# What a product costs on the clock that orders a chain of transformer layers

## The chip, the cores and the metric

The kernel runs on one core of a Trainium2 chip. The metric is the device time of one execution in microseconds (us); the figure given is the median of three executions. TensorE (PE) does the matrix products, VectorE (DVE), ScalarE (ACT) and GpSimd (POOL) the elementwise work, SyncE (SP) issues most of the transfers. Each engine runs its own instructions strictly in the order in which the program was written for it, and waits for other engines by semaphores.

## The reference, cut to what matters

512 tokens of 1024 features pass through two blocks; all of it is in float32.

```
f = swiglu(rms_norm(h)) ;  h += 0.5 * rms_norm(f)            # feed-forward, width 2816
u = rms_norm(h) @ w_in                                        # mixing
h += rms_norm(concat(norm(stick_breaking(u)), norm(chunk_band(u))) @ w_out)
f = swiglu(rms_norm(h)) ;  h += 0.5 * rms_norm(f)
h += rms_norm((p @ w_ple_proj) * sigmoid(h @ w_ple_gate))     # gated embedding (PLE)
x = h
x += conv_mixer(rms_norm(x)) ; x += fox_attention(rms_norm(x))
x += gated_delta_rule(rms_norm(x)) ; x += windowed_attention(rms_norm(x))
return rms_norm(x)
```

The gated delta rule works in chunks of 64 tokens and inverts a triangular 64x64 matrix for each head and chunk. What follows a norm can't start before the sum over all features of the layer before is there; these are the places where the program has a chain of small steps between two large products.

## The kernel before, in words

Activations lie feature-major, 128 features on the partitions and 512 tokens along the columns. Each large product (GEMM) multiplies a 128x128 weight block with up to 512 columns. Weights and activations are split into a high and a low part, so that a float32 product is three products of a faster type; one such triple is the unit in which the GEMM loops (`gemm`, L689; `vproj`, L745) work. A weight block is loaded by SP, its high part is copied out by ACT, its low part subtracted by DVE (`load_to`, L637).

The rest of the network is written as generators. A norm has the steps `stats` (L820: products of one column that sum over partitions, then a square root on ACT and a few small operations on DVE), `rows` (L842: a transpose that spreads the factor over the partitions) and, after a block whose output is normed, `post_norm`: for each of 8 feature tiles a scaling on DVE, a residual addition to `h` on DVE or POOL, a copy on ACT, a split on DVE and a square whose sum POOL or DVE takes. It ends with the next norm's `stats` and `rows`. In what follows, g is the step that scales and adds, g2 the norm behind it; both are done for two halves of 256 tokens. Attention heads and the heads of the delta rule (`head`, L1683) are longer generators of the same kind; the latter's triangular inverse uses products of 32x32 (`mm32`, L1772).

What interleaves all this is a rough clock, kept while the program is written. `free["PE"]` is its time on PE; each product adds its assumed cost there (`product`, L658, called by `mm`, L669, and `transpose`, L684). Operations of the other engines wait in a list and are written when their turn comes by the clock (`next_op`, L336; `Eng.call`, L366 on, holds their assumed costs: a line in the number of columns for each engine). After each triple of GEMM products `poll` (L566) looks at the generators: a generator's next step is written as soon as what it needs has been ready by the clock for 150 ns:

```
if t.ready + MARGIN <= free["PE"]:
    t.step()
```

So the costs decide nothing but order: how many GEMM products stand ahead of a step on PE, and what stands ahead of an operation on DVE, ACT and POOL. Work in products narrower than the array is also counted up (`thin`), and past a limit of 900 ns GEMM products that could run go first.

In the profile nearly all operations of DVE, ACT and POOL have line L391 (the helper that issues them), products L682 and transposes L687.

Of the kernel before, what the change touches and what calls it, by code (L numbers as in the profile page):

```python
# [13 lines left out]
PSUM = bass.MemoryType.PSUM  # L14

# functions of the activation tables, in the order in which they are looked for
TABLES = {0: (AF.Exp, AF.Tanh), 3: (AF.Sqrt,), 5: (AF.Ln,), 6: (AF.Ln, AF.Exp), 9: (AF.Sin,), 18: (AF.Silu, AF.Tanh, AF.Sin)}
P = 128
S = 512
# [3 lines left out]
# tiles whose sums after a norm are taken off the vector engine  # L23
# [7 lines left out]
# column tiles of the delta rule's projections for each head, and the gates projected after them  # L31
GDN_QKV = {j: [m + j for m in (0, 8, 16) if m + j != 1 and j < 8] for j in range(1, 9)}
GDN_Z = {j: [24 + i for i in z] for j, z in zip(range(1, 9), ((), (), (), (0,), (1,), (2,), (3,), (4, 5, 6, 7)))}
# column tiles of the windowed attention: keys, queries and gates
# [4 lines left out]
def _weights_plan():  # L39
    """Order in which the 128x128 weight blocks are used: (weight, k tile, column tile); or a block of the last  # L40
    columns, 32 of each of 4 k tiles: (weight, NARROW, number)."""
# [95 lines left out]
def _constants():  # L137
    """Constants of the shapes: matrices of 128 rows, side by side."""
# [4 lines left out]
    # sums over the later keys, and over the earlier tokens  # L143
# [4 lines left out]
    # joins of blocks of b rows within 32: the odd row blocks at the even column block before  # L148
# [14 lines left out]
class Loan:  # L163
    """Gives a place back when the last view of it is gone."""
# [37 lines left out]
def chain_kernel(ctx, tc, xT, pT, wall, params, consts, chbias, pos, out):  # L202
# [8 lines left out]
    # Each engine runs its instructions in the order of tracing, so that order decides how well they overlap.  # L211
    # A rough clock is kept while tracing. The products are traced as they come and advance it. What the other
    # engines are given waits in `pending` and is traced when its turn comes by that clock: inputs there, engine
    # free. free[e]: when engine e has done what was traced; at[tile][part]: when a part of a tile is there;
    # used[tile][part]: when its last use ends.
# [5 lines left out]
    # what a task's inputs should be there before its products  # L221
    MARGIN = 150.0
    # time of products in parts of the array since others; too many in a row let its clock drop
# [8 lines left out]
    def name(x):  # L232
        """Of the place that a tile is in."""
        return place_of.get(x.name, x.name)

    def parts(ap):
        """The 128-column parts of a tile that are touched, and the elements per partition."""
        w = ap.ap[0][0]
        lo = hi = ap.offset % w if w > 1 else 0
        n = 1  # L240
        for st, c in list(ap.ap)[1:]:
            hi += abs(st) * (c - 1)
            n *= c
        return range(lo // P, hi // P + 1), n

    # from the end of an instruction to the start of one that waits for it
# [8 lines left out]
    def there(ap, key):  # L255
        """When a tile's part can be read by an engine."""
# [5 lines left out]
    def unused(ap, key):  # L262
        """When it can be written."""
# [23 lines left out]
    class Op:  # L287
        """An instruction of an engine other than the tensor engine."""
# [14 lines left out]
        def load(self):  # L303
            """The table to load first."""
# [31 lines left out]
    def next_op():  # L336
        """The pending instruction that can start first, and when."""
# [20 lines left out]
    class Eng:  # L358
# [6 lines left out]
        def __getattr__(self, op):  # L365
            f = getattr(self.eng, op)  # L366

            def call(*a, **kw):
# [19 lines left out]
                else:  # L388
                    a0, a1 = (258, 3.34) if ptr else self.POOL.get(op, (147, 2.1))
                    cost = a0 + a1 * n  # L390
                Op(self.key, lambda: f(*a, **kw), outs, ins, cost, self.prio, func, more)  # L391
# [3 lines left out]
    def both():  # L395
        """Has the table of exp and ln loaded, in its turn."""
# [8 lines left out]
    # for what has time, and for what others wait for  # L405
# [4 lines left out]
    class Places:  # L410
        """Tiles of a size, lent for as long as a view of them is kept."""
# [4 lines left out]
        def close(self):  # L416
            """Gives the free ones back, and each of the others when its loan ends."""
            self.of.free.extend(self.free)
            self.free = self.of.free
# [5 lines left out]
        def take(self, n):  # L425
            """Some of the places, for a task alone."""
# [14 lines left out]
    class Slot:  # L441
        """A place whose tiles differ in type."""
# [22 lines left out]
    def room(n):  # L465
        """Whether a task can take places, with some left for others."""
# [5 lines left out]
    class Row(dict):  # L472
        """Tiles by number, there from their first use on."""
# [20 lines left out]
    # Generators hold chains of products. They yield what their next products wait for: tiles, a number of  # L494
    # banks, another task, a condition. Products of the running GEMM fill that time.
# [5 lines left out]
    def ready_at(y):  # L501
        if y is None:
            return 0.0
        if isinstance(y, int):  # one bank more stays for the GEMM, if it is not the one that waits
# [39 lines left out]
    def go_on(until=NEVER):  # L544
        """The next event: an instruction of another engine or a task's step, if before a time."""
# [20 lines left out]
    def poll(on=None):  # L566
        """Run what is ready; what gets ready until the tiles `on` are there."""
# [38 lines left out]
    def roots():  # L606
        """Has the table of roots loaded before it is needed."""
        A.activation(dull, eps, AF.Sqrt)

# [1 line left out]
    # chunks loaded ahead: more before the engines are busy with norms, and then fewer  # L611
# [7 lines left out]
    def load(i):  # L619
# [3 lines left out]
        if PLAN[i][0][1] == NARROW:  # L623
            # both parts of each k tile's columns side by side
# [6 lines left out]
        # soon needed, or not  # L631
# [36 lines left out]

# [1463 lines left out]
```

## Time and profile before

| | |
|---|---|
| time, median of 3 | 2178.8 us (2176.52 to 2179.45) |
| span of the profiled execution | 2180.4 us (no other time is given for that execution) |
| PE busy | 2125.1 us (97%), 13647 records |
| DVE, ACT, POOL busy | 1310.0 (60%), 991.7 (45%), 291.0 us (13%) |
| mean granted TensorE clock | 0.993 |

The profile shows one execution. "Busy" is the time in which an engine had an instruction under way. In a timeline, neighbouring instructions of one form are joined in a row (x12 is 12 of them); in square brackets stands how long the engine idled before the row and which engine let it go on. The granted clock (PEclk) is 1.00 where TensorE runs at 2.4 GHz and 0.50 where it runs at 1.2 GHz.

### The profile page before, as it was taken

What the parts mean: (1) busy time and instruction counts of PE and PEld (TensorE: products, weight loads), DVE (VectorE), ACT (ScalarE), POOL (GpSimd) and SP (SyncE); (2) the same over time, 40 slices, a digit from 0 to 9 for tenths busy, and PEclk for the clock granted to TensorE, in tenths of its full rate; (3) what the DMA queues carried; (4) which work ended last, traced back from release to release, by engine and by line L of the source; (5) the groups of instructions that cost most, each with busy time, mean ns of one, the idle gap of its engine ahead of it and who ended that gap; (6) DMA issues with size and microseconds to landing.
All of it is one profiled execution on the core that took longest, in us unless ns stands there. A gap on an engine that the chain in (4) does not pass through costs nothing.

```text
span 2180.4 us, 35912 instructions
## 1 busy us (share of the span) xinstructions
PE 2125.1 (97%) x13647; PEld 1783.3 (82%) x13647; DVE 1310.0 (60%) x2755; ACT 991.7 (45%) x2167; POOL 291.0 (13%) x596
## 2 busy tenths in 40 slices
PE   8999999999999999999989999999998999999998
PEld 6888889878889888889988887888877777778777
DVE  5433455757767442455775554256568677665896
ACT  5332343566766332333643234344446554533764
POOL 0000001210103000000120012000015242222320
PEclk9999999999999999999999999999999999999999
DMA  5332241211231332332323223322222212223221
GB/s 168 97 97 94 96 138 58 64 61 55 87 102 45 108 115 74 100 111 79 93 73 97 97 89 112 122 64 67 70 85 69 60 55 55 64 83 89 81 83 59
DMA packets 105405, 186.13 MB, mean 85 GB/s; under 512 B 12392, under 2 KB 18952, under 8 KB 105232
## 3 DMA queue, kind: packets, MB, share of 16 engines
q1 hardware_dynamic: 103920, 179.62, 26.7%
q0 software_dynamic: 1312, 4.21, 0.6%
q8 instruction: 107, 1.75, 0.3%
q14 instruction: 66, 0.54, 0.1%
HBM read 179.03 MB, written 2.13 MB: 83 GB/s over the span
## 4 chain that ended last, share of the span: by engine, by line
PE 83%; DVE 10%; POOL 3%; issue 2%; ACT 2%; DMA 1%; SPq 0%; DVEq 0%; POOLq 0%; ACTq 0%
PE ps L682 81%; DVE t L391 8%; PE ps L687 2%; POOL b L391 2%; ACT t L391 1%; DVE h L391 1%; POOL t L391 1%; DVE b L391 1%; DMA wst<-in_wall_dram 0%; DMA h<-in_xT_dram 0%; ACT L391 0%; DVE pad L391 0%; SPq L391 0%; POOL h L391 0%; DVE a L391 0%
## 5 line engine op out<-in xcount | busy, mean ns | idle before, releaser
L682 PE MATMUL ps<-t,t 128*128 128x512 f32 (+6 forms) x10712 | 2046.1, 353 | 18.3 <-DVE t L391 9.9
L682 PEld LDWEIGHTS ps<-t,t 128*128 128x128 f32 (+2 forms) x10712 | 1684.2, 186 | 320.4 <-issue 28.0
L391 DVE TENSOR_TENSOR t<-wst,t 128x512 fp32r<-128x512 f32 (+1 forms) x646 | 446.7, 717 | 255.9 <-ACT t L391 254.5
L391 ACT ACTIVATE t<-t 128x512 f32<-128x512 f32 (+4 forms) x450 | 248.7, 566 | 614.6 <-DVE t L391 604.2
L391 ACT ACTIVATE t<-wst 128x512 fp32r<-128x512 f32 (+1 forms) x646 | 381.0, 622 | 95.6 <-DMA wst<-in_wall_dram 93.7
L391 DVE TENSOR_TENSOR t<-ps,t 128x512 f32<-128x512 f32 (+2 forms) x247 | 155.4, 639 | 299.9 <-PE ps L682 297.9
L391 DVE TENSOR_TENSOR t<-t,t 128x512 fp32r<-128x512 f32 (+4 forms) x367 | 225.3, 625 | 68.2 <-ACT t L391 62.3
L391 ACT ACTIVATE t<-ps 128x512 f32<-128x512 f32 (+5 forms) x357 | 143.4, 418 | 255.6 <-PE ps L682 171.9
L391 POOL TENSOR_TENSOR t<-t,t 128x512 f32<-128x512 f32 (+1 forms) x99 | 119.9, 1212 | 543.0 <-ACT t L391 464.5
L391 POOL TENSOR_TENSOR h<-h,t 128x256 f32<-128x256 f32 x40 | 34.1, 860 | 798.3 <-DVE t L391 796.7
L391 ACT ACTIVATE t<-t,a 128x257 f32<-128x257 f32 (+5 forms) x128 | 66.2, 519 | 45.2 <-DVE a L391 42.7
L391 ACT ACTIVATE t<-h,prm 128x256 fp32r<-128x256 f32 (+1 forms) x80 | 46.3, 588 | 81.2 <-DVE h L391 70.2
L391 DVE SCALAR_TENSOR_TENSOR t<-h,prm,t 128x256 fp32r<-128x256 f32 (+1 forms) x80 | 65.0, 826 | 8.8 <-ACT t L391 8.8
L391 DVE SCALAR_TENSOR_TENSOR t<-pad,prm,t 128x512 f32<-128x512 f32 (+1 forms) x92 | 68.6, 753 | 0.8
L687 PE MATMUL ps<-cst,t 128*128 128x128 f32 x400 | 63.1, 279 | 2.8 <-DVE t L391 2.0
L391 ACT ACT_TABLE_LOAD x48 | 61.6, 1283 | 6.1 <-DVE a L391 4.5
L687 PEld LDWEIGHTS ps<-cst,t 128*128 128x128 f32 x400 | 48.7, 143 | 15.2 <-DVE t L391 3.3
L391 ACT ACTIVATE t<-h 128x256 f32<-128x256 f32 (+2 forms) x112 | 49.5, 466 | 22.6 <-DVE h L391 20.3
L391 POOL TENSOR_SCALAR b<-b 128x4 f32<-128x4 f32 (+3 forms) x84 | 23.2, 276 | 231.1 <-DVE b L391 226.0
L682 PEld LDWEIGHTS ps<-t 32*32 32x32 f32 (+1 forms) x2304 | 33.1, 109 | 24.4 <-DVE t L391 10.3
L391 DVE TENSOR_SCALAR t<-t,a 128x256 f32<-128x256 f32 (+3 forms) x128 | 49.2, 394 | 2.1
L682 PE MATMUL ps<-t 32*32 32x32 f32 (+1 forms) x2304 | 41.0, 197 | 7.1 <-DVE t L391 6.8
(93 smaller groups left out, 670.6 us busy)
## 6 DMA issues: line engine op xcount, KB each, us to landing
wst<-in_wall_dram SPq DMA_DIRECT2D x644, 256.0 KB, 2.7
t<-t SPq DMA_DIRECT2D x40, 64.0 KB, 2.0
h<-in_xT_dram SPq DMA_DIRECT2D x8, 256.0 KB, 5.3
t<-in_chbias_dram POOLq DMA_DIRECT2D x8, 256.0 KB, 3.1
t<-cdr POOLq DMA_DIRECT2D x8, 256.0 KB, 5.7
t<-gdr SPq DMA_DIRECT2D x32, 64.0 KB, 3.8
out_dram<-t SPq DMA_DIRECT2D x16, 128.0 KB, 1.8
cst<-in_consts_dram SPq DMA_DIRECT2D x1, 626.0 KB, 6.3
```

What stands on the lines that cost most here:

```text
L391: Op(self.key, lambda: f(*a, **kw), outs, ins, cost, self.prio, func, more)
L682: PE.matmul(ps, lhsT, rhs, start=start, stop=stop, **kw)
L687: PE.transpose(ps, src, idn)
```

## The change

No instruction is added or taken out: both programs have the same 11800 products and the same operations on the other engines. What changes is the table of costs by which the clock runs. A product's cost without the new term for array parts:

| product | columns | cost before, ns | cost after, ns |
|---|---|---|---|
| split float32 (GEMM) | 512 | 215.8 | 226.7 |
| split float32 (GEMM) | 256 | 109.2 | 120.0 |
| split float32 | 128 | 215.8 | 226.7 |
| float32 | 128 | 215.8 | 220.0 |
| float32 | 32 | 109.2 | 220.0 |
| transpose | 128 | 107.0 | 110.0 |
| 32x32 of the inverse | 32 | 34 | 25 |

New is `changed`: 95 ns more for a product that uses another part of the array (32, 64 or 128 rows by 32, 64 or 128 columns) than the product before it. On the other engines, an instruction on 32 to 127 partitions costs 115 ns more. Explicit costs (`tile=`) change for the sums of norms, gates, the weighing in attention, the stick-breaking values and the products of the inverse. Comments were taken out as well, and line numbers shift (L391 to L393, L682 to L697, L687 to L702).

```
+                if op != "dma_start" and any(32 <= x.ap[0][1] < P for x in outs + ins):
+                    cost += 115
                 Op(self.key, lambda: f(*a, **kw), outs, ins, cost, self.prio, func, more)
...
+    mode = [(P, P)]
+    CHANGE = 95.0
+
+    def changed(rows, cols):
+        new = tuple(next(x for x in (32, 64, P) if n <= x) for n in (rows, cols))
+        if new == mode[0]:
+            return 0.0
+        mode[0] = new
+        return CHANGE
+
     def mm(ps, lhsT, rhs, start=True, stop=True, tile=None, **kw):
         ps, lhsT, rhs = raw(ps), raw(lhsT), raw(rhs)
-        n = max(parts(rhs)[1], 64)
+        n = parts(rhs)[1]
         if tile is not None:
             ns = tile
         elif rhs.dtype == F32:
-            ns = 4 * n / 2.4 + 2.5
+            ns = 2 * max(110.0, (2 * n + 8) / 2.4)
         elif rhs.dtype == F32R:
-            ns = (n if n >= 256 else 4 * n) / 2.4 + 2.5
+            ns = ((n if n >= 256 else 4 * n) + 32) / 2.4
         else:
-            ns = n / 2.4
+            ns = max(n, P) / 2.4 + 2.5
+        ns += changed(rhs.ap[0][1], parts(lhsT)[1])
         thin[0] = max(0.0, thin[0] + (ns if tile is not None else -0.5 * ns))
...
-        product(ps, (src, idn), 107.0)
+        product(ps, (src, idn), 110.0 + changed(P, P))
...
-                   skip_group_check=True, tile=187)
+                   skip_group_check=True, tile=220)
...
-                       start=j == 0, stop=j == n // P - 1, skip_group_check=True, tile=134 if len(heads) > 1 else None)
+                       start=j == 0, stop=j == n // P - 1, skip_group_check=True, tile=110 if len(heads) > 1 else None)
...
-                       tile=0.95 * (S - kt * P))
+                       tile=0.84 * (S - kt * P))
...
-                        mm(ps[gs, cs], lhsT[gs, cs], rhs[gs, cs], tile=34)
+                        mm(ps[gs, cs], lhsT[gs, cs], rhs[gs, cs], tile=25)
...
-                    mm(p5[b, cs], nL[a, c * P + b.start : c * P + b.stop], Tm[a, cs], tile=34)
+                    mm(p5[b, cs], nL[a, c * P + b.start : c * P + b.stop], Tm[a, cs], tile=40)
...
-                mm(p8[64:P, cs], nL[0:64, c * P + 64 : c * P + P], T64[0:64, cs], tile=50)
+                mm(p8[64:P, cs], nL[0:64, c * P + 64 : c * P + P], T64[0:64, cs], tile=124)
```

How the order moves is counted on PE by the GEMM products that stand ahead of a step, and three places show it. In the names, ps is a PSUM bank, cst the table of constants, b a small tile, h the residual stream, prm the gains and t any other tile; the last number only counts tiles, and differs between the two programs for one and the same tile.

The first place is PE at the end of the first feed-forward layer, first half of the tokens: the `stats` of g2 are the products of one column (128x1).

```order
L682 MATMUL ps_236<-t_7_2929,t_5_2698 128x256
L682 MATMUL ps_237<-t_6_2924,t_5_2698 128x256
L682 MATMUL ps_237<-t_6_2924,t_6_2699 128x256
L682 MATMUL ps_237<-t_7_2929,t_5_2698 128x256
L682 MATMUL ps_241<-t_6_2924,t_5_2698 128x256
L682 MATMUL ps_241<-t_6_2924,t_6_2699 128x256
L682 MATMUL ps_241<-t_7_2929,t_5_2698 128x256
L682 MATMUL ps_239<-cst,t_8_2925 128x1 x2
L682 MATMUL ps_240<-t_6_2924,t_5_2698 128x256
```

```order
L697 MATMUL ps_235<-t_6_2305,t_2_2674 128x256
L697 MATMUL ps_235<-t_6_2305,t_2_2675 128x256
L697 MATMUL ps_235<-t_6_2306,t_2_2674 128x256
L697 MATMUL ps_235<-t_7_2383,t_2_2674 128x256
L697 MATMUL ps_235<-t_7_2383,t_2_2675 128x256
L697 MATMUL ps_235<-t_7_2384,t_2_2674 128x256
L697 MATMUL ps_236<-cst,t_8_2922 128x1 x2
L697 MATMUL ps_235<-t_4_2461,t_2_2674 128x256
L697 MATMUL ps_235<-t_4_2461,t_2_2675 128x256
```

Before, the products of the next layer's first column tiles (t_6_2924, the operand just made) already stand ahead of the sums; after, the last products of the feed-forward layer's second half still follow them. Between the `rows` of g and these `stats` stand 108 products of 256 columns before and 99 after.

The second place is DVE in the second half of the same stretch, just ahead of that half's `stats` of g2: operations out of `wst` are the low parts of weight blocks, those on h and prm the splits of the next operand, and those out of ps with one other tile evacuate products.

```order
L391 TENSOR_TENSOR t_3_3308<-wst_248,t_4_3307 128x512
L391 SCALAR_TENSOR_TENSOR t_7_2952<-h_255,prm,t_9_2943 128x256
L391 SCALAR_TENSOR_TENSOR t_5_3219<-t_4_1608,b_166,ps_235 128x256
L391 SCALAR_TENSOR_TENSOR t_9_2969<-h_256,prm,t_8_2947 128x256
L391 TENSOR_TENSOR t_6_3334<-wst_249,t_6_3333 128x512
L391 SCALAR_TENSOR_TENSOR t_7_3329<-ps_236,t_4_3194 128x256
L391 TENSOR_TENSOR t_8_3330<-ps_237,t_4_3194 128x256
L391 SCALAR_TENSOR_TENSOR t_3_3331<-ps_241,t_4_3194 128x256
L391 TENSOR_TENSOR t_7_3357<-wst_246,t_7_3356 128x512
L391 SCALAR_TENSOR_TENSOR t_4_2975<-h_257,prm,t_9_2960 128x256
```

```order
L393 SCALAR_TENSOR_TENSOR t_7_2949<-h_255,prm,t_9_2940 128x256
L393 TENSOR_TENSOR t_9_3292<-wst_247,t_6_3291 128x512
L393 SCALAR_TENSOR_TENSOR t_4_3213<-t_4_1608,b_166,ps_236 128x256
L393 SCALAR_TENSOR_TENSOR t_9_2966<-h_256,prm,t_8_2944 128x256
L393 TENSOR_TENSOR t_4_3316<-wst_248,t_6_3315 128x512
L393 SCALAR_TENSOR_TENSOR t_4_3337<-ps_237,t_4_3168 128x256
L393 TENSOR_TENSOR t_3_3338<-ps_241,t_4_3168 128x256
L393 SCALAR_TENSOR_TENSOR t_4_2972<-h_257,prm,t_9_2957 128x256
```

One weight subtraction that stood ahead of the last scaling (the operation with b_166) stands behind it now, and one that stood ahead of the last split (h_257) stands behind that.

The third place is PE in the delta rule, where the first 32x32 products of head 0 stand among the GEMM products of the projections.

```order
L682 MATMUL ps_240<-t_33_13897,t_32_14425 128x512
L682 MATMUL ps_240<-t_23_13916,t_36_14526 128x512
L682 MATMUL ps_240<-t_23_13916,t_36_14527 128x512
L682 MATMUL ps_240<-t_22_13917,t_36_14526 128x512
L682 MATMUL ps_235<-t_28_14465 32x32 x16
L682 MATMUL ps_240<-t_21_13919,t_36_14526 128x512
```

```order
L697 MATMUL ps_238<-t_25_13897,t_22_14375 128x512
L697 MATMUL ps_238<-t_23_13916,t_27_14406 128x512
L697 MATMUL ps_238<-t_23_13916,t_30_14407 128x512
L697 MATMUL ps_238<-t_20_13917,t_27_14406 128x512
L697 MATMUL ps_240<-t_36_14451 32x32 x16
L697 MATMUL ps_238<-t_23_13919,t_27_14406 128x512
```

The neighbours look alike, but what stands ahead differs: between the score products of head 1 and these 32x32 products lie 45 GEMM products before and 33 after.

The same count at the other places of which the prediction speaks, as GEMM products by which a step stands earlier than before: in the exit of the first feed-forward layer 3 at its first `rows`, 12 at the first `stats` of g2, 6 at the second `rows` of g, 30 at the second `stats` of g2 and 24 at the last `rows`; in that of the second feed-forward layer 6 at its first step, 6 to 9 at the second half's `stats` and `rows` of g, and 24 at its last `rows`; in that of the gated embedding 3 at its first `rows`, 12 at the `stats` of the second half, and 27 at its last `rows` (all of 256 columns). At the end of the delta rule's output product 3 at the `stats` and 6 at the `rows` (of 512 columns). In the attention stages a step stands earlier by 1.1 us of PE work on average in the mixing layer and by 2 us in the windowed attention, counted with the durations of the trace before.

## Rows read from the trace of the kernel before

**Rows 1.** The page: busy time and share of the span, and the chain that ended last.
```profile
PE 2125.1 (97%) x13647; PEld 1783.3 (82%) x13647; DVE 1310.0 (60%) x2755; ACT 991.7 (45%) x2167; POOL 291.0 (13%) x596
...
PE 83%; DVE 10%; POOL 3%; issue 2%; ACT 2%; DMA 1%; SPq 0%; DVEq 0%; POOLq 0%; ACTq 0%
```

**Rows 2.** Busy time by stretch: PE, PEld, DVE, ACT, POOL, granted clock, DMA.
```profile
200.00:300.00 100.00, 100.00 (x443) 82.81 (x442) 47.43 (x73) 30.16 (x54) 0.00 (x0) 1.00 0.31 100
358.00:405.00 47.00, 43.01 (x351) 41.82 (x350) 37.85 (x87) 24.14 (x57) 22.63 (x28) 1.00 0.25 74
657.00:700.00 43.00, 39.23 (x320) 38.08 (x319) 36.59 (x84) 25.29 (x62) 21.03 (x24) 1.00 0.18 57
1085.00:1126.00 41.00, 34.90 (x275) 34.09 (x274) 35.45 (x81) 23.93 (x52) 19.21 (x24) 0.96 0.18 52
1640.00:1930.00 290.00, 279.09 (x3709) 222.50 (x3709) 201.34 (x509) 148.26 (x475) 99.58 (x271) 0.99 0.23 63
1660.00:1690.00 30.00, 24.52 (x439) 18.31 (x439) 28.25 (x66) 11.10 (x40) 15.94 (x32) 0.93 0.22 63
2050.00:2140.00 90.00, 88.41 (x569) 68.08 (x569) 79.31 (x257) 63.04 (x168) 23.14 (x53) 1.00 0.24 71
```

**Rows 3.** PE's timeline at the exit of the first feed-forward layer.
```profile
361.10 13.19 PE L682 MATMUL ps<-t,t 128*128 128x256 f32 x108
375.36 0.61 PE L682 MATMUL ps<-cst,t 128*128 128x1 f32 x4 [1.07 <-POOL t L391]
...
381.20 0.38 PE L687 MATMUL ps<-cst,b 128*128 128x128 f32 x2
381.33 9.10 PE L682 MATMUL ps<-t,t 128*128 128x256 f32 x73
...
395.59 2.30 PE L682 MATMUL ps<-t,t 128*128 128x256 f32 x17 [1.11 <-DVE t L391]
397.73 0.50 PE L682 MATMUL ps<-cst,t 128*128 128x1 f32 x4
```

**Rows 4.** POOL's timeline in the same stretch.
```profile
395.98 0.73 POOL L391 TENSOR_TENSOR t<-t,t 128x256 f32<-128x256 f32 x1 [0.99 <-ACT t L391]
```

**Rows 5.** DVE's timeline there: a weight subtraction, and a split beside POOL and alone.
```profile
391.51 1.23 DVE L391 TENSOR_TENSOR t<-wst,t 128x512 fp32r<-128x512 f32 x1
392.66 0.95 DVE L391 SCALAR_TENSOR_TENSOR t<-h,prm,t 128x256 fp32r<-128x256 f32 x1
...
397.18 0.47 DVE L391 SCALAR_TENSOR_TENSOR t<-h,prm,t 128x256 fp32r<-128x256 f32 x1
```

**Rows 6.** PE's timeline: second feed-forward exit, embedding exit, end of the delta rule.
```profile
676.55 0.40 PE L687 MATMUL ps<-cst,b 128*128 128x128 f32 x2 [1.79 <-DVE b L391]
...
1093.17 0.60 PE L682 MATMUL ps<-cst,t 128*128 128x1 f32 x4 [1.85 <-DVE t L391]
...
1112.72 6.02 PE L682 MATMUL ps<-t,t 128*128 128x256 f32 x36 [2.16 <-DVE t L391]
...
1968.11 0.65 PE L687 MATMUL ps<-cst,b 128*128 128x128 f32 x4 [2.75 <-POOL b L391]
```

**Rows 7.** PE's timeline in the delta rule, head 0's chain.
```profile
1650.30 11.27 PE L682 MATMUL ps<-t,t 128*128 128x128 f32 x53
1664.06 0.45 PE L682 MATMUL ps<-t 32*32 32x32 f32 x32 [2.49 <-DVE t L391]
...
1688.52 0.45 PE L682 MATMUL ps<-t 32*32 32x32 f32 x32 [2.74 <-DVE t L391]
```

**Rows 8.** PE in stretches of 3.41 us: busy (count), granted clock, DMA.
```profile
1112.61:1116.02 3.41, 3.30 (x15) 0.50 0.18 67
1116.02:1119.43 3.41, 3.41 (x31) 1.00 0.00 0
1593.89:1597.30 3.41, 3.41 (x9) 0.50 0.71 217
1597.30:1600.71 3.41, 3.41 (x18) 1.00 0.06 21
```

More of the change, by code (lines that the diff above doesn't have):

```diff
@@ L1621, in gates @@
             for c in range(4):
-                mm(pt[:, c * 16 : c * 16 + 16], t[0:64, c * P : c * P + P], con("ident32")[0:64, 0:16], tile=187)
+                mm(pt[:, c * 16 : c * 16 + 16], t[0:64, c * P : c * P + P], con("ident32")[0:64, 0:16], tile=220)
             del t
@@ L1817, in head @@
                 cs = slice(32 * c, 32 * c + 32)
-                mm(p7[hi[0], cs], U[hi[0], cs], M5[hi[0], cs], tile=34)
+                mm(p7[hi[0], cs], U[hi[0], cs], M5[hi[0], cs], tile=40)
                 for a, b in zip(lo, hi):
-                    mm(p6[a, cs], M5[b, cs], U[b, cs], tile=34)
+                    mm(p6[a, cs], M5[b, cs], U[b, cs], tile=40)
             V.tensor_copy(blocks(T64[:, 0:256])[hi[0], :, 0:32], blocks(p7[:, 0:P])[hi[0]])
```

## The prediction

> **What bounds the kernel now.** I read the page's busy shares first: PE works 2125.1 of 2180.4 us, and the chain that ended last is 83% PE and 10% DVE [rows 1]. The change keeps every product, so PE's 2125.1 us stay; what can move is the 55.3 us in which PE idles, and the stretches in which its clock is low. Next I cut the span into stretches [rows 2]. Between 200 and 300 us PE has no gap at all: a GEMM that only streams weights hides everything. The idle time sits where a chain of small steps runs on DVE, ACT and POOL: 4.0 us at the exit of the first feed-forward layer, 3.8 at that of the second, 6.1 behind the gated embedding, 10.9 in the delta rule, of which 5.5 lie in the 30 us from 1660 on, where DVE is busy 28.25 of 30. Last I read the timelines of those stretches, to see what each wait ends on [rows 3 to 7], and the clock behind them [rows 8].
>
> **What the change does to the order.** A chain's step is written when its inputs have been there for 150 ns by the clock, so a chain of a given planned length is covered by as many GEMM products as the clock takes for that length. With 256 columns dearer by 120.0 against 109.2, 108 products should become 98; the order has 99 between the `rows` of g and the first `stats` of g2. For 512 columns the factor is 226.7 against 215.8, so that there a step moves by a twentieth.
>
> Is the new cost the truer one? 443 products of 512 columns in 100 us are 225.7 ns each [rows 2], 108 of 256 in 13.19 us are 122 [rows 3]. By the Trainium skill (TensorE: Matmul & The Clock Gate, Back-to-back issue gap) the gap is N/2.4 + 2.5 ns, so 215.8 for 512 columns, which is the old cost; the trace disagrees, with 225.7. By the page's 109 ns for each product of 256 columns the term for the exits below, 5.7, would be 5.1.
>
> But a truer PE cost helps only if the chain's costs are as true. They are not: a split of 256 columns that is charged 396 ns (68 + 1.0417 x 256 + 61) took 0.95 us beside POOL and 0.47 alone [rows 5], and a POOL operation charged 685 ns (147 + 2.1 x 256) took 0.73 to 0.9 [rows 4]. Before, PE and the chain were both charged too little; now only the chain is. PE reaches a step with fewer products ahead of it, and finds its inputs late.
>
> **Exit of the first feed-forward layer.** In the first half PE already waits 1.07 us for POOL at 375.36, after 108 products [rows 3]. With 99 it arrives 9 x 0.122 = 1.1 us earlier, and the chain ends when it did: +1.1. In the second half 114 products stand between the `rows` at 381.20 and the `stats` at 397.73, and 90 after: 24 x 0.122 = 2.9. POOL's last sum there ends at 395.98 + 0.73 = 396.71 [rows 4], so 1.0 is slack: 1.9 left. Against that, DVE now does a weight subtraction of 1.23 us [rows 5] behind the chain's scaling that it did ahead of it, which lets the chain end up to 1.2 earlier: 0.7 to 1.9, taken as 1.3. Sum +2.4. The subtraction pushed back feeds products that already waited (1.11 at 395.59), which is why I take the middle and not the low end.
>
> **Exits of the second feed-forward layer and of the embedding.** From the first step to the last the moves grow from 6 to 24 products and from 3 to 27: 18 x 0.122 = 2.2 and 24 x 0.122 = 2.9. DVE is fuller here (36.6 of 43, 35.5 of 41) than at the first exit (37.9 of 47) [rows 2], so subtractions that go behind the chain count for more; I take off half of one and a whole one: +1.6 and +1.7. All three exits: +5.7; low end 1.1 (only the wait that has no slack today), high end 3.0 + 2.2 + 2.9 = 8.1 (no help from DVE).
>
> **End of the delta rule's output product.** The `rows` at 1968.11 wait 2.75 us for POOL [rows 6], without slack, and stand 6 products of 512 columns earlier: 6 x 0.226 = 1.4, with the `stats` before it as a part of that. +1.5; between 0 and 1.5.
>
> **Attention stages.** In windowed attention PE idles 1.6 of 90 us, with DVE busy 79.3 [rows 2]. Most steps there and in the mixing layer have one to two us of slack (an estimate: the median of the times between the last input's end and the step's start is 1.9), and stand 1.1 to 2 us earlier. DVE's own order moves with them. Nothing in the trace prices this directly; the bounds are 0 (slack covers it) and +8 (the average move, in full, in each of four to five groups of heads). I take +3, nearer to the low end because slack and move are of one size.
>
> **Delta rule.** Between head 1's score products and head 0's first 32x32 products there are 45 GEMM products before and 33 after, and the wait there is 2.49 us at 1664.06; the next long one is 2.74 at 1688.52 [rows 7]. The 2304 products of the inverse are charged 9 ns less each, 20.7 us less of clock in all, while the 319 changes of array part at 95 ns charge 30.3 more, most of it in the same heads: the two almost cancel. PE's work ahead of the first step falls by 2.8 us (16.96 to 14.19, summed from the trace's durations in either order), the DVE work ahead of it by 3.7, since evacuations of the projections go behind the head's chain; ahead of the second it is 12.4 on PE and 12.9 on DVE. DVE is the bound there [rows 2], so these cancel: 0. Bounds: -10.9 (every idle us of the stretch recovered) and +12 (PE's 12.4 counted in full, DVE not followed).
>
> **Clock.** In 3.41 us at a granted clock of 0.50, which is 1.2 GHz, PE does 15 products where it then does 31 at 1.00, and 9 where it does 18 [rows 8]: 1.7 us lost each time. The fall at 1112.6 follows an idle time of 2.16; waits of 1.85 at 1093.17 and 1.79 at 676.55 were followed by none [rows 6]. These two steps move up by 9 products and 3 against the first of their exits, 1.1 and 0.4 us, which brings both above 2.1. Two more falls, +3.4; between 0 and four, 6.8.
>
> The other edits (partial partitions, the single costs) act only through the same order, and are in these counts.
>
> **Sum.** 5.7 + 1.5 + 3 + 0 + 3.4 = 13.6 us. The profiled execution's span, 2180.4, is 1.6 above the median of the runs, 0.07%, so I put the sum on the median: 2178.8 + 13.6 = 2192.4, **2192 us**.
>
> **Rivals.** First, faster: in the delta rule DVE's new order clears the head chains, because DVE's work ahead of a step falls by more than PE's does. For it: 3.7 against 2.8 at the first wait, and DVE's 94% there. Against it: 12.9 against 12.4 at the second, no gain to speak of. Then the stretch's idle time falls from 10.9 to about 3, and the two falls of the clock behind 1664 and 1688 go (2 x 1.7); -11.4. With the exits and the end at 1.1 + 1.5: 2178.8 - 8.8 = 2170. It decides from the point at which DVE, at the 32x32 steps, is done before PE.
>
> Second, no change: the slack of one to two us in attention holds, DVE's order follows at the exits and the clock falls no more often. 1.1 + 1.5 and the delta rule at -2: 2179.
>
> Third, much slower: DVE doesn't follow in the delta rule, +12; with exits 8.1, the end 1.5, attention 8 and four falls 6.8 it is 36 at worst; the first two in full and half of the delta rule, the attention and the falls (13.4) give 2178.8 + 23 = 2202, and the worst 2215.
>
> That the change does nothing at all is excluded: the order differs at hundreds of steps.
>
> **How the numbers follow.** About 0.2%, 4.4 us, is what a measurement of this kernel can tell from no change. My forecast has a chance of 0.45 (its own range 2184 to 2200), the faster rival 0.27, no change 0.17, much slower 0.11. So faster 0.27, within 0.2% 0.17, slower 0.56. The range for 8 in 10 takes in the faster rival's middle and all but the worst of the slowest: 2168 to 2211.
>
> **What would show it.** Right: `stats` of g2 at the first exit waiting about 2.2 us for POOL instead of 1.07; idle time at the three exits about 20 us instead of 14 over the same work; more stretches at a granted clock of 0.50, the first new ones behind the embedding's exit and the second feed-forward layer's; GEMM-only stretches at the same 225.7 ns. Wrong: shorter waits at the first 32x32 products of the heads, with PE's idle time in the delta rule below 5 us; or waits at the exits no longer than before, because DVE or POOL reach the chain's operations sooner. If idle time and falls of the clock together don't account for the difference, the whole way of counting is wrong.

## The result and the profile after

The changed kernel takes 2200.45 us (2198.11 to 2202.1, 4 runs), the kernel before 2177.91 beside it: ratio 1.0099, interval 1.0087 to 1.0112. It is slower by 22.5 us, where 13.6 were forecast; 2200 lies inside the range of 2168 to 2211. The two profiled executions stand 17.1 us apart (spans of 2180.4 and 2197.5); what follows accounts for these 17.1, and the other five lie between one execution and another. The profiled execution of the kernel before was longer than its timed ones (a time is 1.7 us above its span in the runs, so about 2182 us, an estimate); that of the changed kernel has the highest mean clock of its four, 0.990, where the others have 0.989, 0.989 and 0.985.

First the page of the changed kernel: busy time by engine, and below it the core's span with its mean granted clock.

```profile
PE 2132.2 (97%) x13647; PEld 1790.7 (81%) x13647; DVE 1303.7 (59%) x2755; ACT 999.0 (45%) x2171; POOL 291.3 (13%) x596
...
core 0: 2197.5 us, clock 0.990
```

PE's idle time is its span less its busy time, 2197.5 - 2132.2 = 65.3 us against 55.3 [rows 1]: +10.0. PE is also busy 7.1 us longer, with the same 13647 products. The mean clock says why: 0.993 became 0.990, so the time at 0.50 rose from 2 x 0.007 x 2180 = 31 to 2 x 0.010 x 2198 = 44 us, and a product takes twice as long there. Half of 13 is 6.5 of the 7.1. So the slowdown has two parts, 10 us of waiting and 7 of a slow clock behind the waits. ACT has four instructions more (2171, against 2167 in [rows 1]), which are loads of its tables. They are not the cause: the run with 256 columns alone, below, has 2167 and loses 17.6 us, and the slowest kernel of all, n + 58, has 2166.

By stretch the changed kernel shows (columns as in rows 2):

```profile
200.00:300.00 100.00, 100.00 (x443) 82.84 (x442) 47.58 (x73) 30.14 (x54) 0.00 (x0) 1.00 0.31 100
358.00:405.00 47.00, 41.23 (x314) 40.21 (x314) 37.24 (x87) 24.10 (x57) 23.03 (x28) 0.93 0.23 74
1640.00:1930.00 290.00, 278.68 (x3709) 222.25 (x3708) 208.50 (x528) 161.35 (x480) 93.26 (x257) 0.99 0.22 63
2050.00:2140.00 90.00, 87.17 (x552) 67.71 (x551) 77.97 (x243) 63.51 (x164) 26.86 (x53) 1.00 0.26 77
```

Where GEMMs stream, 443 products still take 100 us: the change costs nothing there. At the exit of the first feed-forward layer PE idles 5.8 us of 47 in place of 4.0, the mean clock there is 0.93 in place of 1.00, and 314 products are done in the time of 351 [rows 2].

PE's timeline at that exit shows which step waits (in brackets the idle time before a row and who ended it):

```profile
360.90 12.11 PE L697 MATMUL ps<-t,t 128*128 128x256 f32 x99
374.82 0.61 PE L697 MATMUL ps<-cst,t 128*128 128x1 f32 x4 [1.81 <-POOL t L393]
...
381.08 9.98 PE L697 MATMUL ps<-t,t 128*128 128x256 f32 x79
392.27 1.57 PE L697 MATMUL ps<-t,t 128*128 128x256 f32 x11 [1.20 <-DVE t L393]
395.84 1.02 PE L697 MATMUL ps<-cst,t 128*128 128x1 f32 x4 [2.00 <-POOL t L393]
396.71 4.83 PE L697 MATMUL ps<-t,t 128*128 128x256 f32 x21
```

These are the rows that answer to [rows 3]. 108 products became 99, and the wait for POOL grew from 1.07 to 1.81. In the second half the sums had 1.0 us to spare; now PE waits 2.00 for POOL.

```profile
393.56 2.22 POOL L393 TENSOR_TENSOR t<-t,t 128x256 f32<-128x256 f32 x2
```

POOL ends there at 395.78, against 396.71 before [rows 4]: its chain is 0.9 earlier, while PE gets there 3.9 earlier (at 395.84 - 2.00 = 393.84, against 397.73 in [rows 3]).

Next the clock. The second exit in what follows is the one that the prediction calls the exit of the second feed-forward layer. By the program's order it is that of the mixing layer: the steps at 671.90 to 699.49 us of the kernel before belong to the norm behind the mixing layer's output product, and the weights of the second feed-forward layer come after it. PE alone in stretches, with the granted clock behind the busy time: a stretch of the kernel before in which the clock fell, then for the changed kernel the stretch just before the fall, the fall at the first exit, the stretch after it, and the falls of the second exit and the embedding's.

```profile
426.53:429.94 3.41, 3.41 (x16) 0.50 0.17 67
...
388.47:395.30 6.83, 4.15 (x31) 1.00 0.28 82
395.30:402.13 6.83, 6.29 (x29) 0.50 0.67 228
402.13:408.96 6.83, 6.83 (x59) 1.00 0.00 0
682.02:688.84 6.82, 5.93 (x29) 0.50 0.02 4
1105.27:1112.10 6.83, 6.27 (x29) 0.50 0.25 77
```

In 395.30 to 402.13 PE does 29 products where it does 59 in the next stretch: 3.4 us are lost. In the stretch before PE had been busy 4.15 of 6.83 us. Each of these three falls lasts 6.83 us; the seven of the kernel before lasted 3.41 each, 23.9 us in all. The changed kernel has five more of 3.41, which with the three long ones makes 37.5. (The rest of the 31 and 44 us lies in the last 6 to 7 us of the span, where the clock is low in both.)

The other long waits, at the second exit, the embedding's, the first 32x32 products of the delta rule, a later step of its head 0, and the sums and the `rows` at its end:

```profile
680.25 0.61 PE L697 MATMUL ps<-cst,t 128*128 128x1 f32 x4 [1.88 <-DVE t L393]
...
1105.83 1.01 PE L697 MATMUL ps<-cst,t 128*128 128x1 f32 x4 [2.63 <-DVE t L393]
...
1675.30 0.65 PE L697 MATMUL ps<-t 32*32 32x32 f32 x32 [3.94 <-DVE t L393]
...
1702.95 1.01 PE L697 MATMUL ps<-t 32*32 32x32 f32 x56 [1.65 <-DVE t L393]
...
1974.33 1.05 PE L697 MATMUL ps<-cst,t 128*128 128x1 f32 x8 [3.93 <-POOL t L393]
...
1983.95 0.65 PE L702 MATMUL ps<-cst,b 128*128 128x128 f32 x4 [2.75 <-POOL b L393]
```

The wait at the embedding's `stats` went from 1.85 to 2.63 and the first of the delta rule from 2.49 to 3.94. The one of 2.74 before head 0's fourth joining level is gone; the next step of that head, which joins blocks of 32, waits 1.65 instead [rows 6, 7]. The sums at the delta rule's end waited 2.90 in the kernel before:

```profile
1957.82 1.05 PE L682 MATMUL ps<-cst,t 128*128 128x1 f32 x8 [2.90 <-POOL t L391]
```

### The profile page after: what moved, and what is told of

It is laid out like the page before. It is cut to its first block, busy times and chain, and to the rows that moved or that the text cites. A ratio compares the mean times of both kernels' runs of the same rounds, so it can differ in the third digit from the quotient of the medians.

```text
span 2197.5 us, 35905 instructions
## 1 busy us (share of the span) xinstructions
PE 2132.2 (97%) x13647; PEld 1790.7 (81%) x13647; DVE 1303.7 (59%) x2755; ACT 999.0 (45%) x2171; POOL 291.3 (13%) x596
## 5 line engine op out<-in xcount | busy, mean ns | idle before, releaser
L697 PE MATMUL ps<-t,t 128*128 128x512 f32 (+4 forms) x10712 | 2050.0, 353 | 19.2 <-ACT t L393 9.1
L697 PEld LDWEIGHTS ps<-t,t 128*128 128x128 f32 (+1 forms) x10712 | 1692.1, 187 | 323.4 <-issue 26.6
L393 DVE TENSOR_TENSOR t<-wst,t 128x512 fp32r<-128x512 f32 (+1 forms) x646 | 448.6, 722 | 283.2 <-ACT t L393 281.7
L393 ACT ACTIVATE t<-t 128x512 f32<-128x512 f32 (+4 forms) x450 | 249.7, 566 | 618.7 <-DVE t L393 603.9
L393 ACT ACTIVATE t<-wst 128x512 fp32r<-128x512 f32 (+1 forms) x646 | 381.1, 621 | 96.7 <-DMA wst<-in_wall_dram 93.0
L393 DVE TENSOR_TENSOR t<-ps,t 128x512 f32<-128x512 f32 (+2 forms) x247 | 156.1, 639 | 289.0 <-PE ps L697 286.1
L393 DVE TENSOR_TENSOR t<-t,t 128x512 fp32r<-128x512 f32 (+4 forms) x367 | 225.3, 624 | 80.5 <-ACT t L393 74.2
L393 ACT ACTIVATE t<-ps 128x512 f32<-128x512 f32 (+5 forms) x357 | 143.7, 418 | 263.5 <-PE ps L697 177.3
L393 POOL TENSOR_TENSOR t<-t,t 128x512 f32<-128x512 f32 (+1 forms) x99 | 117.5, 1188 | 541.2 <-ACT t L393 469.6
L393 POOL TENSOR_TENSOR h<-h,t 128x256 f32<-128x256 f32 x40 | 35.7, 900 | 804.7 <-DVE t L393 803.9
L393 ACT ACTIVATE t<-h,prm 128x256 fp32r<-128x256 f32 (+1 forms) x80 | 46.2, 588 | 82.5 <-DVE h L393 70.8
L393 ACT ACTIVATE t<-t,a 128x257 f32<-128x257 f32 (+5 forms) x128 | 66.2, 519 | 34.4 <-DVE a L393 32.5
L702 PE MATMUL ps<-cst,t 128*128 128x128 f32 x400 | 63.0, 277 | 6.8 <-DVE t L393 4.1
L393 DVE SCALAR_TENSOR_TENSOR t<-h,prm,t 128x256 fp32r<-128x256 f32 (+1 forms) x80 | 62.3, 796 | 10.1 <-ACT t L393 10.1
L393 DVE SCALAR_TENSOR_TENSOR t<-pad,prm,t 128x512 f32<-128x512 f32 (+1 forms) x92 | 66.4, 731 | 1.0
L702 PEld LDWEIGHTS ps<-cst,t 128*128 128x128 f32 x400 | 47.4, 141 | 17.7 <-DVE t L393 6.3
L393 ACT ACTIVATE t<-h 128x256 f32<-128x256 f32 (+2 forms) x112 | 49.4, 466 | 25.8 <-DVE h L393 20.2
L697 PEld LDWEIGHTS ps<-t 32*32 32x32 f32 (+1 forms) x2304 | 32.6, 109 | 22.1 <-ACT t L393 7.8
L393 DVE TENSOR_SCALAR t<-t,a 128x256 f32<-128x256 f32 (+3 forms) x128 | 48.8, 390 | 1.5
L393 POOL TENSOR_SCALAR_AFFINE_SELECT t<-t 128x256 f32<-128x256 f32 (+2 forms) x48 | 23.0, 480 | 194.4 <-DVE t L393 106.6
L393 POOL TENSOR_SCALAR b<-b 128x4 f32<-128x4 f32 (+3 forms) x84 | 22.4, 267 | 190.9 <-DVE b L393 185.6
```

The costliest lines, as they stand in the source:

```text
L697: PE.matmul(ps, lhsT, rhs, start=start, stop=stop, **kw)
L702: PE.transpose(ps, src, idn)
```

## The experiments

The theory (A): a dearer GEMM product makes the planned clock run faster against the chains, so their steps are placed among fewer products; the chains on DVE and POOL take longer than charged, PE arrives early and waits, and behind the waits its clock falls. The rivals: the other costs are to blame (B), any new order costs something whatever its direction (C), and some that belong to single runs. All ratios are against the kernel before, run on the same chip.

| kernel | median us | ratio (interval) | PE idle us | mean clock |
|---|---|---|---|---|
| before | 2177.9 to 2180.0 | | 55.3 | 0.993 |
| changed | 2200.5 | 1.0099 (1.0087 to 1.0112) | 65.3 | 0.990 |
| GEMM cost alone | 2205.6 | 1.0121 (1.0105 to 1.0136) | 65.7 | 0.988 |
| all but the GEMM cost | 2178.5 | 0.9996 (0.9987 to 1.0005) | 56.8 | 0.996 |
| 256 columns alone | 2197.2 | 1.0081 (1.0067 to 1.0095) | 62.5 | 0.989 |
| 512 and 128 columns alone | 2185.5 | 1.0028 (1.0017 to 1.0040) | 57.0 | 0.991 |
| changed, margin 1000 | 2205.0 | 1.0114 (1.0100 to 1.0128) | 72.8 | 0.989 |
| changed, margin 1000 in the first part | 2191.6 | 1.0054 (1.0041 to 1.0066) | 59.9 | 0.991 |
| changed, DVE and POOL dearer | 2188.5 | 1.0040 (1.0027 to 1.0053) | 57.4 | 0.990 |
| before, POOL dearer | 2184.2 | 1.0021 (1.0011 to 1.0031) | 55.9 | 0.991 |
| before, n + 58 | 2222.2 | 1.0190 (1.0176 to 1.0204) | 78.4 | 0.984 |
| before, n - 20 | 2173.3 | 0.9970 (0.9958 to 0.9981) | 50.0 | 0.995 |
| before, n - 50 | 2196.9 | 1.0079 (1.0067 to 1.0092) | 60.9 | 0.988 |
| changed, n - 20 | 2185.7 | 1.0026 (1.0016 to 1.0036) | 52.7 | 0.991 |

(PE idle and clock are from each kernel's one profile; idle is span less busy time.)

**The GEMM cost alone, and everything but it.**

```
-            ns = (n if n >= 256 else 4 * n) / 2.4 + 2.5
+            ns = ((n if n >= 256 else 4 * n) + 32) / 2.4
```

> The kernel before with one edit alone: the cost of the split float32 products, (n + 32)/2.4 in place of n/2.4 + 2.5. Theory A (dearer GEMM products bring the chains' steps forward among them, while DVE and POOL, which carry the chains, are charged too little): most of the slowdown, 2190 to 2200 us, and longer waits at the exits of the two feed-forward layers and of the embedding. Theory B (the slowdown comes from the other costs: array parts, partial partitions, the products of the inverse, in the delta rule and the attention): within 4 us of the kernel before, 2174 to 2182.

> The changed kernel with that one cost put back to n/2.4 + 2.5, all other edits kept. Theory A: 2175 to 2187 us, the exits' waits as before. Theory B: 2195 to 2202.

26.2 us slower with it alone, no difference without it. The first is above the upper end of its expectation, and above the 22.5 of the whole change; the intervals of these two ratios overlap, so the difference between them is not shown. At the first exit the one shows the changed kernel's counts and waits, the other those of before; one row of each:

```profile
360.03 12.11 PE L682 MATMUL ps<-t,t 128*128 128x256 f32 x99
373.94 0.61 PE L682 MATMUL ps<-cst,t 128*128 128x1 f32 x4 [1.80 <-POOL t L391]
```

```profile
361.04 13.19 PE L697 MATMUL ps<-t,t 128*128 128x256 f32 x108
375.29 0.61 PE L697 MATMUL ps<-cst,t 128*128 128x1 f32 x4 [1.06 <-POOL t L393]
```

B falls: with the old GEMM cost, array parts, partial partitions and single costs together change nothing that can be measured.

**By width.** `+ (32 if n == 256 else 6)` in one kernel, `+ (6 if n == 256 else 32)` in the other, both on the kernel before.

> The kernel before with (n + 32)/2.4 for products of 256 columns alone (the halves behind a norm), all others as before. Theory A, with the loss at the exits: 2189 to 2200 us. Theory E (the loss comes from the streams of 512 columns, in the mixing attention and the delta rule): 2174 to 2184.

> The kernel before with (n + 32)/2.4 for the split products of 512 and 128 columns and the old cost for those of 256: the counterpart of the run with 256 columns alone, which took 17.6 us of the 26.2 of both. If the two add, +9 us, 2184 to 2192; in the stretches behind the norms no loss, in the delta rule and the attention the rest. Theory E (streams of 512 columns): over 2195. If the norms' exits are all of it: 2176 to 2184.

17.6 and 5.5 us, 23.1 together against 26.2 for both at once; both of E's forecasts missed. In the traces (times between the last products of one layer's weights and the next's) the run with 256 columns loses 10.2 us from the first feed-forward layer's last inner product up to the end of the mixing layer's input projection, 4.5 from there up to the end of the second feed-forward layer and 4.3 up to that of the convolution's input, and gets back 2.4 in the delta rule and 2.6 behind it; the other run loses 8.9 in the delta rule, under 1 in each of those three, and gets back 2.7 behind the delta rule. So most of the loss lies in the three stretches that hold the norms' exits, by the halves of 256 columns, and the streams of 512 cost a smaller part, in the delta rule. That the exits alone carry it is not shown: in the first stretch PE idles 3.3 us more, and the rest comes with the clock, low for 20.5 us in four falls in place of 3.4 in one. Two of the four come at the first exit (376.7 and 397.2 us) and two in the mixing attention behind it (431.3 and 475.7).

**The margin.** `MARGIN = 1000.0` in the changed kernel; then the same with `MARGIN = 150.0` again behind `st = fox_layer(st)`.

> The changed kernel with a margin of 1000 ns in place of 150 before a chain's step is written, so that each step stands some 7 products of 256 columns later. Theory A: the waits at the exits and part of the clock's falls go, 2176 to 2192 us, with less idle time on PE than the 65 us of the changed kernel. Theory C (any new order of so full a kernel costs something, there is no direction in it): 2195 to 2205.

> The changed kernel with the margin of 1000 ns up to the end of the forgetting attention and 150 from the delta rule on. Theory A (steps that follow a norm come too early): the 12 us that the margin gave back up to there in the trace of the run before (1589.4 us against 1601.3) stay, and the delta rule costs what it costs in the changed kernel: 2185 to 2192 us. Theory D (what the margin gave back is taken again later, whatever the later margin): 2198 to 2206.

The first missed A's range: 2205, no gain, at the upper end of what C gave. Its trace says where the gain went. The forgetting attention's last product ends at 1589.4 us, 12 us sooner than in the changed kernel and within 3 of the kernel before; then the delta rule's last head ends after the products that were to cover it, as PE's timeline there shows:

```profile
1955.76 1.11 PE L702 MATMUL ps<-cst,t 128*128 128x128 f32 x4 [6.27 <-DVE t L393]
1958.38 21.94 PE L697 MATMUL ps<-t,t 128*128 128x512 f32 x87 [1.50 <-ACT t L393]
```

A head's chain has many short steps, and each was put off by up to 850 ns more; that this sum is the reason was not tried by itself. With the old margin from there on, 2191.6 us: 9 of the first part's 12 us stay, as A says and D doesn't.

**Truer costs for the chain.** `(147, 2.1)` becomes `(147, 2.9)` for POOL and `1.0417` becomes `1.35` for DVE in the changed kernel; then POOL's alone in the kernel before.

> The changed kernel with DVE and POOL charged as its trace has them: 1.35 ns a column on DVE in place of 1.04 (a split of 256 columns 475 ns) and 2.9 on POOL in place of 2.1 (256 columns 889 ns). Theory A: the chains are charged truly, steps come later, 2172 to 2190 us. Theory C: 2195 to 2205.

> The kernel before with one edit: POOL charged 2.9 ns a column in place of 2.1 (256 columns 889 ns, as the trace has it). Theory A (the chain's costs are too low against PE's): steps behind a norm come later, 2168 to 2178 us, with shorter waits at the three exits. Theory F (only the ratio of PE's cost to everything counts, not the chain's members): 2176 to 2184.

The first gives back 12 of the 22.5 us. The second missed A's range and lies at the upper end of F's: 5.0 us slower. At the first exit it does what A says, 117 products and a wait of 0.61:

```profile
360.87 14.27 PE L682 MATMUL ps<-t,t 128*128 128x256 f32 x117
375.75 0.61 PE L682 MATMUL ps<-cst,t 128*128 128x1 f32 x4 [0.61 <-POOL t L391]
```

But at the second exit PE waits 4.19 us at 687.73 for the factor of the next norm, where before it waited for none, and the clock is low for longer: its seven falls last 34 us in place of 24 (0.991). A cost that is truer for one step moves all that follows; it is no gain by itself.

**The dose.** `(n + 58) / 2.4`, `(n - 20) / 2.4` and `(n - 50) / 2.4` for GEMM products in the kernel before; then n - 20 in the changed kernel.

> The kernel before with GEMM products charged (n + 58)/2.4, dearer than the trace has them. Theory A (each ns more brings the steps further forward): slower still than 2205, 2208 to 2230 us. Theory C (any other order costs about the same): 2195 to 2206.

> The kernel before with GEMM products charged (n - 20)/2.4, 205.0 ns for 512 columns and 98.3 for 256, cheaper than the trace has them. Theory A: the steps come later, the waits at the exits shrink, 2165 to 2180 us, unless the last products run out before a chain does. Theory C: 2190 to 2206.

> The kernel before with GEMM products charged (n - 50)/2.4, 192.5 ns for 512 columns and 85.8 for 256. Theory A has a turning point: steps that come later than their inputs lengthen the chains, and where the products behind them run out PE waits at the end of a layer. 2168 to 2180 us, with less idle time at the norms' exits than at (n - 20) and more at the ends of the delta rule and of the attention. If only lateness counted: under 2170.

> The changed kernel with its cost of split products replaced by (n - 20)/2.4, so its other edits with cheaper GEMM products. Theory A: the two effects add, 2170 to 2176 us (-0.9 and -6.3 from the runs of each alone). Theory C (each new order has its own luck): anywhere from 2165 to 2190.

With 85.8, 98.3, 109.2, 120.0 and 130.8 ns for 256 columns the times are 2196.9, 2173.3, about 2179, 2205.6 and 2222.2: a valley with its floor near 98, below what a product takes (120, from the rows below: (14.27 - 10.67) / 30). The first exit shows the falling side, n + 58 first and n - 20 next:

```profile
360.77 10.67 PE L682 MATMUL ps<-t,t 128*128 128x256 f32 x87
374.71 1.01 PE L682 MATMUL ps<-cst,t 128*128 128x1 f32 x4 [3.27 <-POOL t L391]
```

```profile
363.56 14.27 PE L682 MATMUL ps<-t,t 128*128 128x256 f32 x117
378.67 1.05 PE L682 MATMUL ps<-cst,t 128*128 128x1 f32 x8 [0.84 <-DVE t L391]
```

87, 99, 108, 117 products, waits of 3.27, 1.81, 1.07 and 0.84. The last is no longer for POOL and not for these sums: in that row the second half's first sums come ahead of them, and it is for those that PE waits. C falls as a rule, since n + 58 came out slower and n - 20 faster than it allows: the direction decides. On the other side of the valley, at n - 50, GEMM products themselves wait for operands that a late chain made, and the mixing layer's output product waits for the norm of its input:

```profile
397.31 0.98 PE L682 MATMUL ps<-t,t 128*128 128x256 f32 x6 [3.00 <-DVE t L391]
...
644.19 0.65 PE L687 MATMUL ps<-cst,b 128*128 128x128 f32 x4 [3.08 <-POOL b L391]
```

I had expected the turning point but not its size (2168 to 2180 against 2196.9). n - 20 in the kernel before is the fastest of all, 0.30% below it and 1.2% below the changed kernel. In the changed kernel it is 12 us worse than in the one before, though the other edits alone did nothing. A's forecast, that the two effects add, missed, and C's wide range (2165 to 2190) holds the result: a single order can be off by some 12 us that A does not count. Of the 10.7 us between the two profiles 2.7 are idle time, and the rest comes with the clock (0.991 against 0.995). About half of it is lost by the end of the mixing layer's output product and half in the windowed attention. The first place is the one that waits 3.08 at n - 50:

```profile
632.06 0.65 PE L702 MATMUL ps<-cst,b 128*128 128x128 f32 x4 [2.38 <-POOL b L393]
```

So with these edits n - 20 already shows a wait of the valley's other side. Which of them moves it was not tried.

## Why the prediction was right, point by point

- **What bounds it.** Right: PE's products cost the same, the time turned on PE's idle time and on its clock. The rule by which the order moves, fewer products for the same planned chain, gave 98 for 108; it was 99, and 87 and 117 at other costs.
- **First exit, +2.4.** The first half's wait grew by 0.7, where 1.1 was counted: the chain itself ended 0.3 sooner. In the second half idle time rose from 0.34 + 0.33 + 1.11 to 1.20 + 2.00, by 1.4, where 1.3 was forecast (PE came 3.9 earlier in place of 2.9, having waited less on its way, and the chain 0.9), and the run without the GEMM cost shows the cause. Over the whole stretch it is 1.8, since a wait of 1.14 for the second half's first sums became one of 0.74.
- **The other two exits, +3.3.** Not so in the changed kernel. At the mixing layer's exit the long waits 0.75, 1.79 and 0.57 became 1.88, 0.89 and 1.11, 0.8 more, of which short waits that went give half back: 0.4 over the exit. At the embedding's PE idles 0.7 less. All three exits rose by 1.4, not 5.7. The count of products is not what failed: with the GEMM cost alone almost the same moves make 1.7, 1.4 and 2.1 at the three, 5.2 together. What failed is the overlap: waits and falls of the clock were added, but a fall inside an exit slows PE, which then comes later to the next steps and waits less. At the embedding's exit 126 products lie between the sums of g and the operands below in both of these kernels, and the operands are there 22.7 and 22.2 us after the sums. With the GEMM cost alone PE gets there after 19.2 us and waits 3.48 (first row); in the changed kernel, with the fall of 6.83 on its way, after 21.3, and waits 0.85 (second row). Another 1.2 of idle time came where nothing was counted, in the embedding's gate product behind the second feed-forward layer (1.78 at 1063.38).

```profile
1130.70 1.41 PE L682 MATMUL ps<-t,t 128*128 128x256 f32 x6 [3.48 <-DVE t L391]
```

```profile
1127.99 0.98 PE L697 MATMUL ps<-t,t 128*128 128x256 f32 x6 [0.85 <-DVE t L393]
```

- **Ends of layers, +1.5.** 1.0 at the sums of the delta rule's end, as its `rows` kept 2.75; another 0.6 at the sums after the forgetting attention, which weren't in the count at all.
- **Attention, +3.** About 4 in the traces: 2.9 in the mixing attention, where two transposes wait 0.98 and 0.59 and one 1.37 that waited little before, and 1.2 in the windowed attention.
- **Delta rule, 0.** Nearly: PE idles 1.2 more there, its two longest waits together went from 5.23 to 5.59, and the stretch up to its last input product is 2 us longer. The first rival's reason, that DVE's work ahead of the first step falls by more than PE's, did not decide: that wait grew to 3.94. The charges do not almost cancel, as the prediction has it: the profile has two records for each float32 product, and by the program 1024 products of the inverse (8 heads, 8 groups of 16), not 2304, are charged 9 ns less. That is 9.2 us against the 30.3 more; the forecast of 0 did not use it.
- **Clock, +3.4.** Mis-sized by half. I counted two more falls of 3.41 us; the traces have 37.5 us in falls in place of 23.9, which costs about 7. New are a long fall at the first exit, which was not named, a long one at the second, which was, and one at 1064.3 in the embedding's gate product; the embedding's own fall became a long one; two at the delta rule and its end went. The mark of 2.1 us does not hold: in the kernel before a fall at 426.53 already followed a wait of 1.94, and the same wait of 1.94 was followed by none in the changed kernel (at 430.24). On the medians the clock costs more, an estimate: the changed kernel's runs have 0.989, those of the kernel before beside the experiments 0.994, and a mean clock lower by 0.005 is 11 us of 2180.
- **Sum.** The waiting terms, 5.7 + 1.5 + 3, gave 10.2 and measured 10.0. That they agree is luck: the exits measured 1.4 in place of 5.7, and the rest 8.6 in place of 4.5. The clock was put at 3.4 and measured about 7, so exits and clock together came out near the forecast (8.5 for 9.1), and what was missing lies in the rest. The direction and the way (fewer products ahead of a step, waits, a low clock behind them) were right, the size of most parts was not. The time lies at the upper end of my own range (2184 to 2200) and nearer to the third rival's 2202 than to 2192, but that rival's ground, 6 us in the delta rule, did not show.
- **The duration of a product.** Rows of 117 and of 87 products differ by 14.27 - 10.67 us, so one takes 120 ns; the prediction's 122 takes in the end of each row's last product. The 5.1 that it gives for 109 ns scales the whole term; with its own subtractions kept, it would be 4.7.

The formula of the Trainium skill (TensorE: Matmul & The Clock Gate, Back-to-back issue gap), which that section gives for a single isolated product, makes 215.8 ns for 512 columns and 109 for 256. The traces, where each product has its own weight load, disagree: 225.7 for 512 columns (442 or 443 products between 200 and 300 us in all fourteen) and 120 for 256.

So the new cost of a product is the truer one, and still lost. The reading that fits is that the old table's error on PE hid a larger one on DVE and POOL. It is shown in part: truer costs there give back 12 of the 22.5 us, and not the rest.

## What to carry to other kernels

A planner's costs are tuned as a set: correcting the one that is wrong can bring out the others that were wrong in the same direction, so compare the ratio of the bounding engine's cost to that of the chains, and sweep it. Count, at each place where the bounding engine waits, how much work stands ahead of the step before and after: at the first exit 9 products fewer predicted a wait to within half a microsecond, and over the three exits, with the GEMM cost alone, such counts gave 5.7 us for 5.2. Price a new wait with the clock that falls behind it, which here came to about 70% on top of all waiting; but do not add both in full at one place, since PE at half speed reaches the next steps later.

## What the runs showed of the hardware

A wait of PE costs more than its length once the clock falls. A fall of 3.41 us lost about 1.7, one of 6.83 about 3.4 (29 products, and 59 in the stretch after it). In the kernel before all seven falls lasted 3.41, behind waits of 1.94 to 2.90. In the changed one five lasted 3.41 and three 6.83, and the length of the wait does not tell which: 3.94 was followed by 3.41 (at 1675.30), 1.20 and 2.00 by 6.83 (at 395.30), and 1.94 by a fall in one kernel and none in the other. What sets the long ones apart in these two traces is that PE still waited after the clock had fallen: the falls at 395.30, 682.02 and 1105.27 had waits that ended 0.5, 2.1 and 0.6 us into them, the others none that ended more than 0.1 us into them. It is no rule: with 256 columns alone a fall at 397.18 lasted 6.83 behind a wait that had ended at 397.13.

Over the fourteen kernels the mean clock goes from 0.984 to 0.996, which is about 70 to 17 us at half speed, and it follows idle time only loosely: 52.7 us of idle at 0.991, 56.8 at 0.996.
